# Layer 0 of a two-layer diffusion block: background sums moved into the merge, splits of two k tiles at a time, another order of the first eight blocks, an output product in five parts

## The chip, the cores and the metric

The kernel runs on one core of a Trainium2 chip. The metric is the device time of one execution in microseconds (us), the median over the runs shown. The core has TensorE (PE, matmuls), VectorE (DVE), ScalarE (ACT), GpSimd (POOL) and SyncE (SP); each works through a queue of its own in order, and SP's queue issues nearly all DMAs.

## The reference, cut to what matters

Two layers over 512 latent tokens and 256 context tokens of width 1024; the context goes through layer 0 in full and in layer 1 gives only keys and values. In each layer:

```
mod = silu(cond) @ w_mod[l] + b_mod[l]                      # six sections of 1024, for c and for c_ctx
h   = rms_norm(x) * (1 + scale1) + shift1
...                                                          # projection, conv mixer, attention, gMLP
x   = x + gate1 * (g_a*y_a + g_b*y_b + g_c*y_c) @ w_o        # the merge, then w_o
h2  = rms_norm(x) * (1 + scale2) + shift2
x   = x + gate2 * (silu(h2 @ w_ff1) * (h2 @ w_ff3)) @ w_ff2  # width 2816 = 22 tiles of 128
```

## The kernel before, in words

Everything is stored with the width on the 128 partitions and the tokens along the free axis, so an activation is eight k tiles of 128 x 768 in layer 0 (tokens 0 to 511 latent, XS; 512 to 767 context, CS) and of 128 x 512 in layer 1. Every GEMM keeps f32 accuracy by splitting both sides into a high and a low part: ACT casts the high part (`wh`, or the first half of `A`, `B`, `u`, `z`), and POOL or DVE subtracts it from the source for the low part (`split`, L223 to L225). A k tile costs three matmuls (`mm`, L227 to L235). A weight piece of 128 x 512 comes by one DMA on SP into `ws` (5 buffers), then becomes `wh` and `wl` (4 buffers each).

**Background sums.** The modulation vectors are sums over `w_modT`: one 512 KB tile (`wm`, 3 buffers) by DMA, then one DVE pass for each condition (`mod_sums`, L151 to L157), so two for the 32 tiles of layer 0's sections 2 to 5 and the first 16 of layer 1, and one for the last 32. They are called a few at a time by `pump`. A tiny POOL copy from a result of the place where the sum was called (`gate_mods`, L180) into the `wm` buffer holds the DMA back until that result exists.

**Merge, w_o, norm.** The merge takes eight output tiles j (`merge_b`, L821 to L830), with three sums behind each. The product with w_o (`wo_j`, L849 to L866) does tiles 0 to 3 over all 768 tokens, with two sums behind each, then tiles 4 to 7 over the token half 0 (0 to 383) and again over half 1 (384 to 767), so that the norm of half 0 runs while half 1 is multiplied (`lagged`, L417 to L431). `norm_half` (L400 to L415) writes the normed half as `Y` tiles (DVE multiplies, ACT adds the shift), and splits each into `A`.

**FF.** The first two of the 22 width tiles (`first_pair`, L898 to L924) are eight blocks of 24 matmuls: width tile n (0, 1), factor i (0 for w_ff1, 1 for w_ff3), half t. Its order is, written n,i,t: 000, 010, 001, 011, 100, 110, 101, 111. Beside it DVE forms sums and differences of `Y` (`pair_forms`, L282 to L297: `tf`, split into `B`), which the other ten pairs of width tiles need. Such a pair is `ff_pair` (L926 to L970): two products of seven matmul blocks in place of eight (`pair_product`), with weights that DVE adds up first (`fw`, L263), each product followed by one sum. The output product `ff2_j` (L985 to L1001) is taken in six parts of the width, 2, 4, 4, 4, 4 and 4 tiles; each part adds its product into the residual `xr` (DVE, L990) for all eight output tiles j. After each odd j a sum is called. In the last part, tiles j 0 to 3 run over all tokens, then 4 to 7 over XS, then 4 to 7 over CS, and the norm of layer 1 follows.

The order of the instructions on each engine is laid down when the kernel is built, by a scheduler that simulates a timeline; it differs from the order of the code.

Of the kernel before, what the change touches and what calls it, by code (L numbers as in the profile page):

```python
# [36 lines left out]
def dit_block(ctx: ExitStack, tc: tile.TileContext, xT, conds, vecs, ident_in, rope_c, rope_s,  # L37
# [27 lines left out]

# [210 lines left out]
    def half_of(k, t):  # L276
        return pair_at(8 * (k // 2) + 4 * t + 2 * (k % 2))

    def sum_of(i, kk):
        return pair_at(32 + 8 * i + 2 * kk)  # L280

    def pair_forms(Y, kk):  # L282

        b11, b12, b21, b22 = Y[kk, 0], Y[kk, 1], Y[kk + 4, 0], Y[kk + 4, 1]

        def form(x, y, op):
            t = slot("tf", HT)
            nc.vector.tensor_tensor(t, x, y, op=op)
            return t
        if kk % 2 == 0:  # L290
            new_arena(*range(8 + kk // 2, 16, 2))
# [108 lines left out]
    def norm_half(X, G, S, t, Y):  # L400

        a, b = t * HT, (t + 1) * HT
        RB = norm_stats(X, a, b)
        yield
        if t == 0:
            for kk in range(4):
                Y[kk, 0], Y[kk, 1], Y[kk + 4, 0], Y[kk + 4, 1] = four("Y")
        for k in (0, 4, 1, 5, 2, 6, 3, 7):
            y = Y[k, t]
            for u, v, c in kinds(a, b):  # L410
                nc.vector.scalar_tensor_tensor(y[:, u - a:v - a], X[k][:, u:v], G[:, k, c:c + 1], RB[:, u - a:v - a],
                                               op0=ALU.mult, op1=ALU.mult)
                nc.scalar.activation(y[:, u - a:v - a], y[:, u - a:v - a], AF.Identity, bias=S[:, k, c:c + 1])
            split(y, *half_of(k, t), nc.vector if k % 2 else nc.gpsimd)
            yield  # L415
# [45 lines left out]
    for l in range(2):  # L461
# [387 lines left out]
        def wo_j(j, sg):  # L849
# [48 lines left out]
        def first_pair(U):  # L898
# [14 lines left out]

            for n in range(2):
                for t in range(2):
                    for i in range(2):
                        if t == 0:
                            ww[n, i] = load_w(w_13[l, i, n], KD)
                        go(n, i, t)
                    if n == 1:  # L920
                        pair_forms(Y2, 2 * t)
                        pair_forms(Y2, 2 * t + 1)
# [48 lines left out]

        parts = [(0, 8), (8, 15), (15, 22)] if last else [(0, 2), (2, 6), (6, 10), (10, 14), (14, 18), (18, 22)]
        for pi, (f0, f1) in enumerate(parts):
# [11 lines left out]
            def ff2_j(j, sg):  # L985
# [87 lines left out]
```

## Time and profile before

| | us |
|---|---|
| median of the runs | 1975.67 (1975.33 to 1978.29, 3 runs) |
| the profiled execution's own time | 1975.22 |
| its span in the profile | 1973.4 |
| PE busy | 1879.8 (95% of the span) |
| DVE busy | 1164.6 (59%) |
| ACT busy | 747.8 (38%) |
| POOL busy | 859.9 (44%) |

The stages that the change touches, on the profile's clock: the merge from about 340 to 573 us, w_o from 573 to 643, `first_pair` to 693, the FF pairs and the output parts to 1183, then the norm of layer 1, whose first matmul starts at 1193. PE's busy share is the figure to start from; the places where PE waits or runs at a lower clock are read from the rows further down.

### The profile page before, as it was taken

Reading aid. Unit: us, or ns where it says so; the run is one execution under the profiler, and the core shown is the slowest. Engines: PE = TensorE matmul, PEld = TensorE weight load, DVE = VectorE, ACT = ScalarE, POOL = GpSimd, SP = SyncE. Lnnn points to the kernel's source line nnn. Section 1 sums busy time; section 2 is a strip of 40 time slices with the busy share of each in tenths; the row PEclk is TensorE's granted clock in tenths of the full one; section 3 lists DMA queues with packets and bytes.
Section 4 is the critical chain, followed back from the end, with each engine's and each line's share of the span. In section 5 each row is a group of like instructions: output and inputs, shape, how many; then the busy total and the mean of one; then the engine's idle time right before and its main releaser. Section 6 shows DMA issues by size and latency. Waiting matters only on the chain.

```text
span 1973.4 us, 27588 instructions
## 1 busy us (share of the span) xinstructions
PE 1879.8 (95%) x10150; PEld 1654.6 (84%) x10150; DVE 1164.6 (59%) x1936; ACT 747.8 (38%) x1459; POOL 859.9 (44%) x722
## 2 busy tenths in 40 slices
PE   5789999999999899999999998999999999999999
PEld 3578998888889789899999987888888888888887
DVE  7877865535359887877676867549523362322222
ACT  4346765222223623232322345448533352313121
POOL 4678743534334415152433347854333253424232
PEclk9989999999999899999999998999999999999999
DMA  8933201324255142323323354410322433332311
GB/s 280 306 101 97 76 27 39 134 76 149 75 185 195 38 144 91 129 91 118 119 95 134 119 183 153 135 34 5 107 90 92 147 108 127 100 102 86 111 43 66
DMA packets 107735, 222.42 MB, mean 113 GB/s; under 512 B 12368, under 2 KB 19792, under 8 KB 107600
## 3 DMA queue, kind: packets, MB, share of 16 engines
q1 hardware_dynamic: 105536, 217.51, 33.0%
q10 hardware_dynamic: 2064, 3.15, 0.6%
q8 instruction: 80, 1.31, 0.3%
q14 instruction: 55, 0.45, 0.1%
HBM read 212.74 MB, written 5.24 MB: 110 GB/s over the span
## 4 chain that ended last, share of the span: by engine, by line
PE 73%; DVE 14%; issue 4%; ACT 3%; DMA 3%; POOL 2%; ACTq 0%; SPq 0%; DVEq 0%; POOLq 0%
PE wide L234 33%; PE pD L234 21%; PE pD L311 5%; PE wide L311 5%; PE pF L234 3%; DMA wm<-in_w_modT 2%; DVE wm L156 2%; PE pO L765 2%; DVE wl L225 2%; PE pPT L759 1%; PE wide L733 1%; DVE junk L156 1%; DVE nm L737 1%; DVE nacc L352 1%; DVE ptl L762 1%
## 5 line engine op out<-in xcount | busy, mean ns | idle before, releaser
L225 POOL TENSOR_TENSOR wl<-ws,wh 128x512 fp32r<-128x512 f32 (+2 forms) x338 | 484.4, 1445 | 462.5 <-ACT wh L224 376.0
L234 PE MATMUL wide<-A,wh 128*128 128x512 f32 (+2 forms) x1728 | 469.3, 367 | 17.4 <-ACT A L224 8.2
L234 PEld LDWEIGHTS wide<-A,wh 128*128 128x128 f32 x1728 | 302.8, 192 | 72.7 <-ACT A L224 10.2
L224 ACT CAST wh<-ws 128x512 fp32r<-128x512 f32 (+2 forms) x536 | 302.2, 607 | 65.4 <-issue 17.5
L234 PE MATMUL wide<-A,wl 128*128 128x512 f32 (+2 forms) x864 | 289.1, 366 | 4.9 <-POOL wl L225 4.9
L225 DVE TENSOR_TENSOR wl<-ws,wh 128x512 fp32r<-128x512 f32 (+1 forms) x198 | 168.4, 851 | 131.5 <-ACT wh L224 121.5
L234 PE MATMUL pD<-A,wh 128*128 128x512 f32 (+1 forms) x784 | 238.2, 384 | 6.6 <-ACT A L224 2.8
L156 DVE SCALAR_TENSOR_TENSOR wm<-wm,fixed 128x1024 f32<-128x1024 f32 x112 | 152.1, 1361 | 49.4 <-DMA wm<-in_w_modT 47.5
L234 PEld LDWEIGHTS wide<-A,wl 128*128 128x128 f32 x864 | 154.2, 192 | 30.7 <-POOL wl L225 6.3
L234 PEld LDWEIGHTS pD<-A,wh 128*128 128x128 f32 x784 | 147.3, 193 | 35.0 <-ACT A L224 3.2
L234 PE MATMUL wide<-u,wh 128*128 128x512 f32 (+1 forms) x600 | 149.5, 352 | 0.9 <-DVE xr L990 0.9
L234 PE MATMUL pD<-A,wl 128*128 128x512 f32 (+1 forms) x392 | 148.7, 382 | 0.0
L234 PE MATMUL pD<-u,wh 128*128 128x512 f32 (+1 forms) x456 | 118.2, 357 | 0.0
L234 PEld LDWEIGHTS wide<-u,wh 128*128 128x128 f32 x600 | 98.9, 188 | 17.3 <-DVE xr L990 1.2
L742 POOL TENSOR_SCALAR pp<-pp,nm 128x768 f32<-128x768 f32 (+1 forms) x80 | 66.8, 836 | 101.2 <-DVE nm L741 65.5
L225 POOL TENSOR_TENSOR u<-su,u 128x768 fp32r<-128x768 f32 (+1 forms) x44 | 72.4, 1655 | 85.2 <-ACT u L224 85.2
L803 ACT ACTIVATE gate<-wide 128x512 f32<-128x512 f32 (+1 forms) x56 | 26.7, 516 | 199.8 <-PE wide L234 199.2
L156 DVE SCALAR_TENSOR_TENSOR junk<-wm,fixed 128x1024 f32<-128x1024 f32 x48 | 68.2, 1420 | 54.3 <-DMA wm<-in_w_modT 47.2
L809 DVE SCALAR_TENSOR_TENSOR gate<-gate,pD 128x512 f32<-128x512 f32 (+1 forms) x45 | 25.6, 596 | 122.4 <-PE pD L234 99.8
L224 ACT CAST wh<-fw 128x512 fp32r<-128x512 f32 x80 | 48.5, 615 | 121.8 <-DVE fw L263 106.3
L224 ACT CAST u<-su 128x768 fp32r<-128x768 f32 (+1 forms) x44 | 31.7, 728 | 165.7 <-DVE su L885 93.9
L234 PE MATMUL wide<-u,wl 128*128 128x512 f32 (+1 forms) x300 | 89.4, 351 | 0.0
(248 smaller groups left out, 3827.0 us busy)
## 6 DMA issues: line engine op xcount, KB each, us to landing
ws<-in_w SPq DMA_DIRECT2D x252, 256.0 KB, 3.8
wm<-in_w_modT SPq DMA_DIRECT2D x112, 512.0 KB, 4.3
ws<-in_w_in SPq DMA_DIRECT2D x184, 256.0 KB, 2.9
ws<-in_w_o SPq DMA_DIRECT2D x48, 256.0 KB, 5.4
ws<-in_w_abc SPq DMA_DIRECT2D x32, 256.0 KB, 2.7
ws<-in_w_six SPq DMA_DIRECT2D x16, 192.0 KB, 4.5
xr<-in_xT SPq DMA_DIRECT2D x8, 384.0 KB, 7.6
ws<-in_w SPq DMA_DIRECT2D x16, 192.0 KB, 2.4
```

Of the source, the lines that this page charges most:

```text
L156: nc.vector.scalar_tensor_tensor(o, t, 1.0, sbc[:, c, :], op0=ALU.mult, op1=ALU.mult, accum_out=MOD[l][:, sec, b, c:c + 1])
L224: nc.scalar.copy(hi, src)
L225: (lo_eng or nc.gpsimd).tensor_tensor(lo, src, f(hi), op=ALU.subtract)
L234: nc.tensor.matmul(d[:, :b - a], lhsT=ww, rhs=aa[:, a:b], start=kk == 0 and i == 0, stop=kk == n - 1 and i == 2)
L311: nc.tensor.matmul(D, lhsT=x[:, kk * P:(kk + 1) * P], rhs=a, start=kk == 0 and i == 0, stop=kk == 3 and i == 2)
L352: nc.vector.tensor_tensor(acc[:, :n], acc[:, :n], sq[:, :n], op=ALU.add)
L733: nc.tensor.matmul(D[:, a - k0:b - k0], lhsT=q[:, c * P - q0:(c + 1) * P - q0], rhs=kt[:, a:b], start=i == 0, stop=i == 1)
L737: nc.vector.tensor_reduce(nm[:, 0:1], D[:, :nk], axis=AX.X, op=ALU.max, negate=True)
L742: nc.gpsimd.tensor_scalar(pt[:, :nk], pt[:, :nk], nm[:, 3:4], 0.0, op0=ALU.mult, op1=ALU.add)
L765: nc.tensor.matmul(o[:, 0:256], lhsT=v3[:, kt, :], rhs=pp[:, j * 256:(j + 1) * 256], start=gi == 0 and j == 0 and i == 0, stop=gi == len(k ...
L803: nc.scalar.activation(g_[:, a:e], D, AF.Tanh, scale=0.5)
L809: nc.vector.scalar_tensor_tensor(g_[:, a:e], g_[:, a:e], 1.0, D, op0=ALU.add, op1=ALU.mult)
```

## The change

The diff, cut to its core (line numbers after it are two to seven higher than before: L910 of before is L914 after, L990 is L992, L413 is L419, L374 is L378):

```diff
@@ pair_forms, norm_half: two k tiles at a time @@
+    def split_two(t, u, eng):
+        d = arena[u // 4].rearrange("p (v h n) -> p h v n", h=2, n=HT)
+        split(t, d[:, 0], d[:, 1], eng)
...
-        t0 = form(b11, b12, ALU.subtract)
-        t1 = form(b22, t0, ALU.add)
-        t2 = form(b22, b12, ALU.subtract)
-        t3 = form(b21, t1, ALU.subtract)
-        for i, t in enumerate((t0, t1, t2, t3)):
-            split(t, *sum_of(i, kk), nc.vector)
+        nc.vector.tensor_tensor(ta, y[:, 0:4:3], y[:, 1:2].to_broadcast([P, 2, HT]), op=ALU.subtract)
+        nc.vector.tensor_tensor(tb[:, 0], y[:, 3], ta[:, 0], op=ALU.add)
+        split_two(ta, 32 + 8 * kk, nc.vector)
+        nc.vector.tensor_tensor(tb[:, 1], y[:, 2], tb[:, 0], op=ALU.subtract)
+        split_two(tb, 36 + 8 * kk, nc.vector)
...
-            split(y, *half_of(k, t), nc.vector if k % 2 else nc.gpsimd)
+            split_two(y4[:, t:4:2], 8 * kk + 4 * t, nc.vector if kk % 2 else nc.gpsimd)
@@ merge_b @@
-                pump(3)
+                pump(4)
@@ wo_j @@
-            if j < 4 and not last:
-                gate_mods[0] = Xn[j][:, W - 1:W]
-                pump(2)
@@ first_pair @@
-            for n in range(2):
-                for t in range(2):
-                    for i in range(2):
...
-                keep_u(su[n], U)
-                pump()
+            for n, i, t in ((0, 0, 0), (0, 1, 0), (1, 0, 0), (0, 0, 1), (0, 1, 1), (1, 0, 1), (1, 1, 0), (1, 1, 1)):
+                if t == 0:
+                    ww[n, i] = load_w(w_13[l, i, n], KD, "xx" if (n, i) == (1, 0) else "hl")
+                go(n, i, t)
...
@@ output product @@
-        parts = ... [(0, 2), (2, 6), (6, 10), (10, 14), (14, 18), (18, 22)]
+        parts = ... [(0, 4), (4, 8), (8, 12), (12, 16), (16, 22)]
...
-                if not last and j % 2:
+                if not last and f1 < NFF:
                     gate_mods[0] = X[j][:, W - 1:W]
                     pump()
...
-                lagged(ff2_j, segs, halves, lambda p: norm(X, G1[1], MOD[1][:, 0], *p, hnext))
+                lagged(ff2_j, segs, halves, lambda p: norm(X, G1[1], MOD[1][:, 0], *p, hnext), KD)
```

So all 32 tiles of layer 0's sums run in the merge, none in w_o and `first_pair`; behind each of the first four output parts stand eight sums in place of four, and behind the last none; the last part runs all eight j over XS first, then all eight over CS, and loads its weights for each. A fourth kind of weight tile (`wx`, 4 buffers) holds the piece that the third block of `first_pair` needs. The matmuls are the same in number and shape.

What this moves in the order of the engines is shown at three places. First ACT's queue in `first_pair`, where the L910 or L914 rows end a block of factor 0 (they read its PSUM bank), the L413 or L419 rows add the shift to `Y` tiles of half 1, and `A`, `B` and `wh` are casts. Before:

```order
L224 CAST A_5671<-Y_6219 128x384
L224 CAST B_6662<-tf_6682 128x384
L224 CAST wh_6590<-ws_6588 128x512
L224 CAST B_6663<-tf_6684 128x384
L224 CAST wh_6596<-ws_6594 128x512
L224 CAST wh_6627<-ws_6625 128x512
L224 CAST B_6664<-tf_6686 128x384
L910 ACTIVATE su_6453<-wide0_72 128x384
L224 CAST wh_6633<-ws_6631 128x512
```

After the change, the same stretch:

```order
L224 CAST A_5714<-Y_6216 128x2x384
L419 ACTIVATE Y_6217<-Y_6217,fixed_74 128x256
L419 ACTIVATE Y_6217<-Y_6217,fixed_74 128x128
L419 ACTIVATE Y_6217<-Y_6217,fixed_74 128x256
L914 ACTIVATE su_6438<-wide0_72 128x384
L419 ACTIVATE Y_6218<-Y_6218,fixed_74 128x128
L419 ACTIVATE Y_6218<-Y_6218,fixed_74 128x256
```

Before, the L910 shown is that of the first block over half 1, behind half 1's last `A` cast, and no L910 stands among half 1's shifts; after, the L914 of the third block over half 0 stands among them, and a cast of `A` or `B` takes two k tiles (128x2x384).

Second, DVE's queue around the end of the first output part, where L990 or L992 adds into `xr`, L156 is a sum (`wm` and `junk` are the two conditions of a tile), and `fw` and `wl` belong to the weights of the next pair. Before, after the part of two tiles:

```order
L990 SCALAR_TENSOR_TENSOR xr_6073<-pD_6941,fixed_74,xr_6073 128x512
L990 SCALAR_TENSOR_TENSOR xr_6073<-pD_6942,fixed_74,xr_6073 128x256
L156 SCALAR_TENSOR_TENSOR wm_6835,fixed_74<-wm_6835,fixed_74 128x1024
L156 SCALAR_TENSOR_TENSOR junk_6886,fixed_74<-wm_6883,fixed_74 128x1024
L990 SCALAR_TENSOR_TENSOR xr_6073<-wide0_72,fixed_74,xr_6073 128x512
L990 SCALAR_TENSOR_TENSOR xr_6073<-wide0_72,fixed_74,xr_6073 128x256
L225 TENSOR_TENSOR wl_7002<-fw_6999,wh_7001 128x512
L225 TENSOR_TENSOR wl_7012<-fw_7009,wh_7011 128x512
L225 TENSOR_TENSOR wl_7016<-fw_6993,wh_7015 128x512
L156 SCALAR_TENSOR_TENSOR wm_6883,fixed_74<-wm_6883,fixed_74 128x1024
L156 SCALAR_TENSOR_TENSOR junk_6932,fixed_74<-wm_6929,fixed_74 128x1024
L263 TENSOR_TENSOR fw_7019<-fw_6999,ws_6991 128x512
```

After the change, at the end of the part of four tiles:

```order
L992 SCALAR_TENSOR_TENSOR xr_6073<-wide1_73,fixed_74,xr_6073 128x512
L992 SCALAR_TENSOR_TENSOR xr_6073<-wide1_73,fixed_74,xr_6073 128x256
L156 SCALAR_TENSOR_TENSOR wm_7193,fixed_74<-wm_7193,fixed_74 128x1024
L156 SCALAR_TENSOR_TENSOR junk_7236,fixed_74<-wm_7233,fixed_74 128x1024
L992 SCALAR_TENSOR_TENSOR xr_6073<-pD_7323,fixed_74,xr_6073 128x512
L992 SCALAR_TENSOR_TENSOR xr_6073<-pD_7324,fixed_74,xr_6073 128x256
L225 TENSOR_TENSOR wl_7386<-fw_7383,wh_7385 128x512
L225 TENSOR_TENSOR wl_7390<-fw_7367,wh_7389 128x512
L156 SCALAR_TENSOR_TENSOR wm_7233,fixed_74<-wm_7233,fixed_74 128x1024
L156 SCALAR_TENSOR_TENSOR junk_7274,fixed_74<-wm_7271,fixed_74 128x1024
L263 TENSOR_TENSOR fw_7393<-fw_7373,ws_7365 128x512
L328 TENSOR_TENSOR tp_7403<-tp_7403,pD_7417 128x384
```

Behind the part's last evacuation seven passes of sums follow within the pair before, and nine after the change; ahead of it stand five before and eleven after.

Third, DVE's queue at the end of layer 0: L352 or L356 adds squares, `ms` and `RR` are the norm's factors, and L374 or L378 writes the normed tiles of layer 1. Before:

```order
L990 SCALAR_TENSOR_TENSOR xr_6073<-pD_11551,fixed_74,xr_6073 128x256
L352 TENSOR_TENSOR nacc_11571<-nacc_11571,nsq_11585 128x256
L357 TENSOR_SCALAR ms_11453<-pst_11448 128x4
L352 TENSOR_TENSOR nacc_11571<-nacc_11571,nsq_11588 128x256
L352 TENSOR_TENSOR nacc_11571<-nacc_11571,nsq_11591 128x256
L357 TENSOR_SCALAR ms_11597<-pst_11594 128x2
L362 COPY RR_11457<-rr_11455 128x512
L156 SCALAR_TENSOR_TENSOR wm_11493,fixed_74<-wm_11493,fixed_74 128x1024
L362 COPY RR_11601<-rr_11599 128x256
L374 SCALAR_TENSOR_TENSOR ny_11464<-xr_5684,fixed_74,pRB_11459 128x512
L374 SCALAR_TENSOR_TENSOR ny_11469<-xr_5684,fixed_74,pRB_11459 128x512
L374 SCALAR_TENSOR_TENSOR ny_11498<-xr_5837,fixed_74,pRB_11459 128x512
```

After the change:

```order
L992 SCALAR_TENSOR_TENSOR xr_5862<-wide1_73,fixed_74,xr_5862 128x256
L356 TENSOR_TENSOR nacc_11581<-nacc_11581,nsq_11586 128x256
L992 SCALAR_TENSOR_TENSOR xr_5862<-pD_11430,fixed_74,xr_5862 128x256
L225 TENSOR_TENSOR wl_11486<-ws_11483,wh_11485 128x512
L378 SCALAR_TENSOR_TENSOR ny_11317<-xr_5733,fixed_74,pRB_11312 128x512
L378 SCALAR_TENSOR_TENSOR ny_11322<-xr_5733,fixed_74,pRB_11312 128x512
L378 SCALAR_TENSOR_TENSOR ny_11359<-xr_5862,fixed_74,pRB_11312 128x512
L378 SCALAR_TENSOR_TENSOR ny_11364<-xr_5862,fixed_74,pRB_11312 128x512
L356 TENSOR_TENSOR nacc_11581<-nacc_11581,nsq_11589 128x256
L225 TENSOR_TENSOR wl_11519<-ws_11516,wh_11518 128x512
L992 SCALAR_TENSOR_TENSOR xr_5993<-wide1_73,fixed_74,xr_5993 128x256
L992 SCALAR_TENSOR_TENSOR xr_5993<-pD_11495,fixed_74,xr_5993 128x256
```

Before, all L990 rows are through ahead of the first normed tile; after, L992 rows of the CS pass (128x256) stand before and behind the normed tiles of XS, with the low parts of the pass's weights between them.

## Rows read from the trace of the kernel before

**Rows 1.** The page's first line.
```profile
span 1973.4 us, 27588 instructions
```

**Rows 2.** Stretches: length, then each engine's busy us (instructions), granted clock, DMA.
```profile
core 0: us, PE busy (x) PEld busy (x) DVE busy (x) ACT busy (x) POOL busy (x), PEclk, DMA share, GB/s
340.00:573.00 233.00, 233.00 (x1322) 202.27 (x1322) 100.26 (x147) 53.84 (x108) 97.20 (x83) 1.00 0.31 108
600.00:627.00 27.00, 25.49 (x146) 24.03 (x145) 27.00 (x42) 7.79 (x15) 13.74 (x9) 1.00 0.77 263
643.30:692.80 49.50, 41.64 (x202) 37.75 (x202) 39.78 (x77) 28.72 (x68) 21.01 (x15) 0.90 0.11 34
674.00:680.00 6.00, 5.79 (x18) 5.79 (x19) 6.00 (x7) 0.87 (x2) 4.28 (x4) 0.50 0.12 21
680.00:692.80 12.80, 12.80 (x75) 12.80 (x74) 8.00 (x17) 4.92 (x12) 1.65 (x2) 0.99 0.23 84
717.40:725.00 7.60, 7.60 (x35) 7.60 (x36) 7.60 (x13) 2.10 (x4) 1.21 (x2) 0.78 0.47 142
775.00:809.00 34.00, 34.00 (x198) 30.07 (x197) 21.95 (x36) 6.46 (x11) 13.16 (x13) 1.00 0.32 109
1178.00:1182.00 4.00, 4.00 (x34) 3.87 (x33) 4.00 (x7) 1.99 (x4) 2.12 (x1) 1.00 0.80 267
1193.30:1199.50 6.20, 6.06 (x15) 4.36 (x16) 6.20 (x8) 4.46 (x7) 5.58 (x7) 0.54 0.41 120
```

**Rows 3.** Waits of PE, 573 to 693 us: total, times, longest.
```profile
PE wide L234 <- POOL wl L225: 3.1, 2, 2.5
PE wide L234 <- ACT A L224: 2.4, 1, 2.4
PE wide L234 <- DVE xr L861: 1.5, 1, 1.5
```

**Rows 4.** Groups of ACT by line, 643 to 693 us and whole run.
```profile
L224 ACT CAST A<-Y 128x384 fp32r<-128x384 f32 x14 | 6.9, 501 | 0.0
L224 ACT CAST B<-tf 128x384 fp32r<-128x384 f32 x16 | 7.8, 510 | 4.2 <-DVE tf L288 4.1
L224 ACT CAST u<-su 128x768 fp32r<-128x768 f32 x22 | 18.1, 836 | 71.8 <-POOL su L952 27.8 <-PE wide L311 20.4 <-PE pD L311 11.9
```

**Rows 5.** Waits of PE, 693 to 1150 us.
```profile
PE wide L311 <- DVE xr L990: 3.4, 1, 3.4
PE pD L311 <- DVE wl L225: 2.4, 1, 2.4
PE pD L311 <- DVE tp L330: 2.2, 2, 1.1
```

**Rows 6.** Groups of DVE by shape, and SP's queue at 805 us.
```profile
L156 DVE SCALAR_TENSOR_TENSOR junk<-wm,fixed 128x1024 f32<-128x1024 f32 x48 | 68.2, 1420 | 54.3 <-DMA wm<-in_w_modT 47.2 <-PE wide L234 6.6 <-issue 0.5
L225 DVE TENSOR_TENSOR wl<-ws,wh 128x512 fp32r<-128x512 f32 x194 | 166.7, 860 | 130.7 <-ACT wh L224 120.8 <-issue 9.3
L263 DVE TENSOR_TENSOR fw<-fw,ws 128x512 f32<-128x512 f32 x40 | 38.2, 955 | 0.3
L990 DVE SCALAR_TENSOR_TENSOR xr<-wide,fixed,xr 128x512 f32<-128x512 f32 x41 | 30.6, 747 | 55.7 <-PE wide L234 55.7
805.51 9.88 SPq L153 DMA_DIRECT2D wm<-in_w_modT  x3
```

**Rows 7.** Timeline of PE at the end of layer 0: start, us.
```profile
1176.70 0.39 PE L234 MATMUL pD<-u,wl 128*128 128x512 f32 x1
1182.73 0.28 PE L234 MATMUL pD<-u,wl 128*128 128x256 f32 x1
1193.27 0.80 PE L234 MATMUL wide<-A,wh 128*128 128x512 f32 x1 [2.30 <-ACT A L224]
```

**Rows 8.** Timeline of DVE and POOL at 617 us.
```profile
618.09 1.77 DVE L225 TENSOR_TENSOR wl<-ws,wh 128x512 fp32r<-128x512 f32 x1
617.10 2.21 POOL L225 TENSOR_TENSOR wl<-ws,wh 128x512 fp32r<-128x512 f32 x1 [2.16 <-ACT wh L224]
```

More of the change, by code (lines that the diff above doesn't have):

```diff
@@ L203, in wtile, with load_w, load_piece @@
         return wp.tile([P, 512], F32 if kind == "s" else F32R, tag="w" + kind, name="w" + kind,
-                       bufs={"s": 5, "h": 4, "l": 4}[kind])
-    def load_w(src, nk):
+                       bufs={"s": 5, "h": 4, "l": 4, "x": 4}[kind])
+    def load_w(src, nk, kinds="hl"):
         res = []
         for k0 in range(0, nk, 4):
-            res += load_piece(src[:, k0:min(k0 + 4, nk), :].rearrange("p k n -> p (k n)"))
+            res += load_piece(src[:, k0:min(k0 + 4, nk), :].rearrange("p k n -> p (k n)"), kinds)
         return res
-    def load_piece(src):
+    def load_piece(src, kinds="hl"):
         n = src.shape[1]
@@ L218, in load_piece @@
         nc.sync.dma_start(st[:, :n], src)
-        hi, lo = wtile("h"), wtile("l")
+        hi, lo = wtile(kinds[0]), wtile(kinds[1])
         split(st[:, :n], hi[:, :n], lo[:, :n], eng)
@@ L276, in half_of, with two_forms @@
     def half_of(k, t):
-        return pair_at(8 * (k // 2) + 4 * t + 2 * (k % 2))
+        return pair_at(8 * (k % 4) + 4 * t + 2 * (k // 4))
     def sum_of(i, kk):
-        return pair_at(32 + 8 * i + 2 * kk)
+        return pair_at(32 + 8 * kk + 4 * (i % 2) + 2 * (i // 2))
+    def split_two(t, u, eng):
+        d = arena[u // 4].rearrange("p (v h n) -> p h v n", h=2, n=HT)
+        split(t, d[:, 0], d[:, 1], eng)
     def pair_forms(Y, kk):
[L284 to L291, printed above, removed]
-        t0 = form(b11, b12, ALU.subtract)
-        t1 = form(b22, t0, ALU.add)
-        t2 = form(b22, b12, ALU.subtract)
-        t3 = form(b21, t1, ALU.subtract)
-        for i, t in enumerate((t0, t1, t2, t3)):
-            split(t, *sum_of(i, kk), nc.vector)
+        y = Y[kk].rearrange("p (b n) -> p b n", n=HT)
+        new_arena(8 + 2 * kk, 9 + 2 * kk)
+        def two_forms():
+            t = big.tile([P, 2 * HT], F32, tag="tf", name="tf", bufs=2)
+            return t.rearrange("p (b n) -> p b n", n=HT)
+        ta = two_forms()
+        nc.vector.tensor_tensor(ta, y[:, 0:4:3], y[:, 1:2].to_broadcast([P, 2, HT]), op=ALU.subtract)
+        tb = two_forms()
+        nc.vector.tensor_tensor(tb[:, 0], y[:, 3], ta[:, 0], op=ALU.add)
+        split_two(ta, 32 + 8 * kk, nc.vector)
+        nc.vector.tensor_tensor(tb[:, 1], y[:, 2], tb[:, 0], op=ALU.subtract)
+        split_two(tb, 36 + 8 * kk, nc.vector)
     def four(name):
@@ L406, in norm_half @@
             for kk in range(4):
[L407 to L413, printed above, removed]
-            split(y, *half_of(k, t), nc.vector if k % 2 else nc.gpsimd)
+                Y[kk] = big.tile([P, 4 * HT], F32, tag="Y", name="Y", bufs=PAIRS["Y"])
+        for kk in range(4):
+            y4 = Y[kk].rearrange("p (b n) -> p b n", n=HT)
+            for k in (kk, kk + 4):
+                y = y4[:, 2 * (k // 4) + t]
+                for u, v, c in kinds(a, b):
+                    nc.vector.scalar_tensor_tensor(y[:, u - a:v - a], X[k][:, u:v], G[:, k, c:c + 1],
+                                                   RB[:, u - a:v - a], op0=ALU.mult, op1=ALU.mult)
+                    nc.scalar.activation(y[:, u - a:v - a], y[:, u - a:v - a], AF.Identity, bias=S[:, k, c:c + 1])
+                yield
+            split_two(y4[:, t:4:2], 8 * kk + 4 * t, nc.vector if kk % 2 else nc.gpsimd)
             yield
@@ L912, in go @@
                     nc.vector.tensor_tensor(o, o, D, op=ALU.mult)
-            for n in range(2):
-                for t in range(2):
-                    for i in range(2):
[L917 to L922, printed above, removed]
-                keep_u(su[n], U)
-                pump()
+            for n, i, t in ((0, 0, 0), (0, 1, 0), (1, 0, 0), (0, 0, 1), (0, 1, 1), (1, 0, 1), (1, 1, 0), (1, 1, 1)):
+                if t == 0:
+                    ww[n, i] = load_w(w_13[l, i, n], KD, "xx" if (n, i) == (1, 0) else "hl")
+                go(n, i, t)
+                if t == 1 and i == n:
+                    for kk in (2 * n, 2 * n + 1):
+                        pair_forms(Y2, kk)
+                if t == i == 1:
+                    keep_u(su[n], U)
         def ff_pair(m, U):
@@ L970, in ff_pair @@
             pump()
-        parts = [(0, 8), (8, 15), (15, 22)] if last else [(0, 2), (2, 6), (6, 10), (10, 14), (14, 18), (18, 22)]
+        parts = [(0, 8), (8, 15), (15, 22)] if last else [(0, 4), (4, 8), (8, 12), (12, 16), (16, 22)]
         for pi, (f0, f1) in enumerate(parts):
```

2 rows, old and new, of the table BUFS are left out of this document.

## The prediction

> **What bounds the kernel now.** I read the page first. The span is 1973.4 us [rows 1], and the profiled execution's own time, 1975.22, is 1.8 us more and 0.45 below the median of 1975.67, so what the sum moves in the span I take off 1975.22. PE is busy 95% of it, so PE is the bound almost everywhere: through the whole merge it has no gap, 233.00 of 233.00 us [rows 2]. A gain can come only from the places where PE waits or runs at a lower clock, and I looked for them stage by stage among the stages that the change touches.
>
> Three are worth the search. First, `first_pair`: 49.50 us [rows 2] for 192 matmuls. Near its end PE runs 75 of them in 12.80 us, 0.171 each [rows 2], so 192 need 32.8 and 16.7 us are lost. Waits for a weight's low part (3.1 us in all) and for `A` (2.4) are the largest named [rows 3]; and from 674 to 680 us the granted clock was 0.50, half of full speed, right behind the longest wait: 18 matmuls took 5.79 us in place of 3.1 [rows 2], 2.7 lost. Second, the end of layer 0: the last context matmul starts at 1182.73, the first matmul of layer 1 at 1193.27 [rows 7], and from there to 1199.50 the clock is 0.54 [rows 2]. Third, the FF pairs from 693 to 1150: the largest waits are 3.4, 2.4 and 2.2 (two of 1.1) [rows 5]; three more of about 1 us each bring them to 10.8, and behind the first the clock is 0.78: 35 matmuls took 7.60 us [rows 2] in place of 6.0, 1.6 lost. Together 12.4.
>
> **The change part by part.**
>
> *Merge.* Eight sums move in, one to each j, two DVE passes of 1.42 each [rows 6], 22.7 us. DVE is busy 100 of 233 us there [rows 2], so it has the room, and PE's unbroken 233 us of matmuls, 29 to a j, are the cover. The fourth sum's POOL copy waits for one of three `wm` buffers, for about one tile's two passes; behind it on POOL stand the low parts of the next j's weights, and behind its DMA on SP that j's pieces, both with a j of PE in front of them. If that cover fails, a PSUM evacuation waits for one pass or two: 0 to 22.7 us. PE has no gap at all with three sums behind each j, which is nearest to 0. I take 0.
>
> *w_o.* Eight sums leave, 22.7 us of DVE. From 600 to 627 us DVE was busy 27.00 of 27.00 [rows 2], and PE waited 1.5 us for one of its w_o evacuations [rows 3]. That wait goes: -1.5.
>
> *first_pair.* The first block over half 1 cannot end before half 1 is normed and split, whatever stands in front of it. Before, it was block 3, and five blocks of 24 x 0.171 = 4.1 us followed, 20.5, plus the wait and the clock (2.5 [rows 3] and 2.7), so it ended at about 692.8 - 25.7 = 667 us. After, a third half-0 block fills the wait, and four blocks follow: -4.1. The splits help a little: a cast of 2 x 384 should cost ACT 0.84 (its cast of 768) in place of 2 x 0.50, so half 1 has 4 x 0.17 = 0.7 us less of ACT, and `B`, 8 x 0.18 = 1.5 [rows 4]. Against it, `wx` adds nothing (the same pieces), but the next pair starts right behind this stage, where before the output part of two tiles gave DVE 18 us to finish `B`. So a wait at the pair's start is new; I give it 1.5 and count it under FF. The clock may well fall at the starved block as it does now. I take -3.5, between -0.5 (the wait is only moved) and -8 (the wait and the half clock go too). With w_o: -5.0.
>
> *FF pairs and output parts.* One part fewer saves DVE eight evacuations of 512 and of 256 (0.75 [rows 6] and some 0.47), 9.8 us, and PE the wait behind the two-tile part (3.4 [rows 5] plus 1.6 of clock). But each part now releases eight sums where it released four, on a DVE that is busy 21.95 of 34 us in such a part already [rows 2]. Four more two-pass sums are 11.4 us: 33 of 34 behind the first part, so what comes late spills into the next pair. There the order has nine passes behind the last evacuation, 12.8 us, ahead of or among weights (a pair product needs five `fw` at 0.96 and about six `wl` at 0.86 [rows 6], 10 us) against a pair product of 84 matmuls, 14.4 us of PE at 0.171. Before, seven such passes cost 3.4 + 1.6; nine, behind a longer part, cost I think 5.5 (3 to 9). The next three transitions have one-pass sums, 1.5 each (0 to 3). With 2.2 of waits for `tp` that I leave, and the 1.5 at the first pair, that is 13.7 against 12.4: +1.3. Bounds -5 and +8.
>
> *End of layer 0.* Before, 10.5 us lay between the last context matmul and layer 1 [rows 7], and the 15 matmuls to 1199.50 took 6.06 us [rows 2] where 15 x 0.226 = 3.4 would do (one of 512 and one of 256 columns take 34.00/99 = 0.343 at full clock, one of 256 takes 4.00/34 = 0.118 [rows 2]): 2.7 more, 13.2 together. After, the context pass is eight j of 18 matmuls at 0.118 us, 17.0 us behind the last XS evacuation, and the norm of XS runs under it; before, only 6 us of it did. The chain from the last XS matmul (1176.70) to layer 1's first took 16.6 [rows 7], which 17.0 just covers. What stays: the statistics' own matmuls, a wait for `RR`, a wait or two for weights whose parts stand behind normed tiles in DVE's and ACT's queues, some clock. I take 4.7 of 13.2, so -8.5. The context pass now loads weights of its own, 16 pieces by 16 DMAs, each cast and subtracted; if that slows it, all but 4 of the gain goes; if nothing waits, it is -12.
>
> Sum: 0 - 5.0 + 1.3 - 8.5 = -12.2, so **1963.0 us**.
>
> **A rule weighed against the trace.** A DVE subtraction of a `wl` that began at 618.09 beside a POOL subtraction (617.10 to 619.31) took 1.77 us against a mean of 0.86, and ended about half a microsecond behind it [rows 8, 6]. The Trainium skill's "SBUF — State Buffer", section "Who interferes with whom", says that a DVE instruction with two SBUF inputs and a GpSimd instruction that reads SBUF shut each other out for the whole instruction. The trace agrees. By that rule the longer splits on POOL hold DVE longer at a time, which is rival C.
>
> **The rivals.** *A, the sums pile up behind the output parts (slower).* The place is SP's queue: at 805.51 it took 9.88 us to issue three gated `wm` loads, with the next pair's weights behind them [rows 6], and the wait for a `wl` of 2.4 in that pair [rows 5] came of it. With eight sums there can be two or three such batches ahead of a weight piece, at four transitions. If each puts 9.88 us on PE, FF goes to 39.5 - 12.4 = +27.1 and the time to 1975.22 - 13.5 + 27.1 = 1988.8. It decides from (13.5 + 12.4)/4 = 6.5 us at a transition. Against it, DVE in such a part has 12 us free, and SP's wait of 9.88 cost PE only 2.4 us and one wait under 1. Chance 0.13.
>
> *B, the end of layer 0 gives little*, since ACT and DVE must make 16 weight pieces' parts and eight normed tiles in the same 17 us: gain 4 there, 1967.5; with half of FF's loss bound added, 1971. For it speaks that DVE was already busy 4.00 of 4.00 us at 1178 to 1182 [rows 2]; against it, its sums leave that stretch. Chance 0.18.
>
> *C, POOL's double splits hold DVE.* In `norm_half` half 1 gives POOL two splits of 2 x 384. At 2.21 us for 512 columns [rows 8], one of 768 columns is 3.3 us (estimate, in proportion); two of them in front of `B` on DVE put `B` and the first pair 6.6 us back: 1969.6. Against it, the forms have four blocks of PE, 16 us, in front of them. Chance 0.06.
>
> *D, more than I count:* the half clock and the 2.5 us wait in `first_pair` go, FF gains 5: 1963 - 4 - 6 = 1953. Chance 0.18. *E, nothing moves*, because what is covered in one place comes back in the next (DVE's work is the same but for 10 us): within 4 us of 1975. Chance 0.08. The forecast itself (1958 to 1968): 0.37.
>
> **The numbers.** About 0.2%, 4 us, is what a measurement can tell from no change. Forecast, D, C and nearly all of B lie more than 4 us below 1975.67: faster 0.77. E and a rest of B: same 0.10. A: slower 0.13. The range leaves out the far half of A and the tail beyond D: 1951 to 1976. The forecast's own is 1958 to 1968.
>
> **What would show it.** PE unbroken in the merge; no wait for w_o's evacuations; the span from the end of w_o to the first pair's first matmul some 4 us shorter, with one wait in it for half 1; a PE wait for `wl` or `fw` in the second pair, behind the part of four tiles, of 3 to 9 us, and none behind a two-tile part; the gap between the last context matmul and layer 1's first under 3 us, at a clock near 1. I am wrong if waits of PE after the four output parts sum to more than 20 us, if the context pass at the end takes well over 17 us, or if the merge shows gaps.

## The result and the profile after

| | before | after |
|---|---|---|
| median of the runs, us | 1975.5 (1974.44 to 1978.29, 4 runs) | 1953.21 (1951.87 to 1953.39, 4 runs) |
| ratio to before | | 0.9884, 95% interval 0.9866 to 0.9901 |
| span of the profiled execution | 1973.4 | 1950.0 |

The change made the kernel 22 us faster; 12.2 were forecast. 1953.2 lies in the range of 1951 to 1976, near its low end, and outside the forecast's own 1958 to 1968. To see where the 22 us came from I cut both profiled executions at the same matmuls (the start of a row in PE's timeline to the start, or for a last matmul the end, of another):

| stage, us | before | after | difference | forecast |
|---|---|---|---|---|
| up to the first matmul of w_o | 573.15 | 572.23 | -0.9 | 0 (merge) |
| w_o, to the first matmul on `A` | 70.16 | 68.20 | -2.0 | -1.5 |
| first_pair, to its last matmul | 49.65 | 41.73 | -7.9 | -3.5 |
| FF, to the last context matmul | 490.05 | 488.73 | -1.3 | +1.3 |
| gap to layer 1's first matmul | 10.26 | -0.17 | -10.4 | -8.5, this row and the next |
| start of layer 1, to the attention's first transpose | 125.68 | 127.32 | +1.6 | |
| from there to the end | 654.45 | 651.96 | -2.5 | 0 |

(The gap is negative since PE's rows overlap: the last context matmul is put down to end at 1170.89, and the next starts at 1170.72.) The first and the last row hold no instruction that the change moves out of its place on PE. Over the profiles of all fourteen kernels here the first lay between 572.2 and 575.8 (but for m8, below) and the last between 651.8 and 655.3, so some 3.5 us in each is what one execution differs from another by. In the kernels that leave them as the change has them, w_o repeats within 0.2 us and `first_pair` within 0.7, while the start of layer 1 lay between 126.2 and 129.3 in the seven kernels without a gap, so its +1.6 says little. The stages between the first row and the last give 20.0 us.

The page of the changed kernel: span, busy time with share and instructions, and the clock in 40 slices.

```profile
span 1950.0 us, 27698 instructions
...
PE 1868.8 (96%) x10150; PEld 1644.1 (84%) x10150; DVE 1178.3 (60%) x1910; ACT 750.5 (38%) x1455; POOL 868.6 (45%) x724
...
PEclk9989999999999999999999999999999999999999
```

PE is busy 11 us less than before for the same 10150 matmuls, its mean granted clock being 0.994 in place of 0.986, and it waits 12 us less. The stretches that answer to [rows 2], in the same columns:

```profile
core 0: us, PE busy (x) PEld busy (x) DVE busy (x) ACT busy (x) POOL busy (x), PEclk, DMA share, GB/s
340.00:573.00 233.00, 233.00 (x1324) 202.12 (x1323) 129.11 (x177) 53.37 (x106) 109.68 (x90) 1.00 0.35 124
600.00:627.00 27.00, 27.00 (x157) 26.20 (x156) 10.89 (x19) 10.76 (x23) 6.86 (x6) 1.00 0.23 82
640.40:682.00 41.60, 37.17 (x206) 34.30 (x204) 38.95 (x56) 24.35 (x47) 14.32 (x9) 1.00 0.10 32
674.00:680.00 6.00, 6.00 (x37) 6.00 (x36) 5.87 (x8) 1.67 (x3) 0.71 (x1) 1.00 0.01 3
757.00:800.00 43.00, 38.83 (x217) 37.46 (x218) 43.00 (x65) 15.56 (x27) 15.51 (x11) 1.00 0.35 117
1150.00:1170.70 20.70, 19.03 (x157) 18.62 (x156) 17.88 (x29) 13.29 (x28) 12.99 (x15) 1.00 0.64 199
1170.70:1177.00 6.30, 5.88 (x27) 4.52 (x26) 6.29 (x7) 4.04 (x8) 4.81 (x4) 1.00 0.81 269
```

The merge is as unbroken as before with 29 us more of DVE; from 600 to 627 us DVE has 10.89 us to do in place of 27.00; and PE runs 674 to 680 at full clock with 37 matmuls in place of 18. The waits of PE that answer to [rows 3], and under the dots to [rows 5]:

```profile
engine line waited for: us in total, times, longest us
PE wide L234 <- ACT su L914: 1.5, 2, 0.8
PE wide L234 <- POOL A L225: 1.3, 2, 0.6
PE pst L359 <- DVE nacc L356: 0.9, 1, 0.9
...
PE pD L315 <- DVE wl L225: 4.6, 4, 1.5
PE wide L315 <- DVE wl L225: 0.9, 1, 0.9
```

No wait in `first_pair` is over 1 us; before, there were two over 2. The waits for w_o's evacuation, for `tp` and behind the two-tile part are gone, and those for `wl` stand in their place, all but one in the second and third pair behind `first_pair`. There DVE is busy 43.00 of 43.00 us (757 to 800, above).

When the norm's factors reach PSUM (`pRB`), half 0 and then half 1, before:

```profile
638.46 0.49 PE L365 MATMUL pRB<-fixed,RR 128*128 128x128 f32 x3
654.68 0.49 PE L365 MATMUL pRB<-fixed,RR 128*128 128x128 f32 x3
```

After:

```profile
634.02 0.49 PE L369 MATMUL pRB<-fixed,RR 128*128 128x128 f32 x3
652.43 0.49 PE L369 MATMUL pRB<-fixed,RR 128*128 128x128 f32 x3
```

Half 0 is ready 4.4 us earlier and half 1 2.3 (0.9 us of each lies ahead of w_o). Last, PE's timeline at the end of layer 0, to be held against [rows 7]: the last XS matmul, two waits in the context pass, and the first matmul of layer 1.

```profile
1149.73 0.39 PE L234 MATMUL pD<-u,wl 128*128 128x512 f32 x1
...
1165.48 0.39 PE L234 MATMUL wide<-u,wl 128*128 128x256 f32 x1 [0.85 <-DVE wl L225]
1168.71 0.39 PE L234 MATMUL pD<-u,wl 128*128 128x256 f32 x1 [0.82 <-DVE wl L225]
...
1170.72 0.63 PE L234 MATMUL wide<-A,wh 128*128 128x512 f32 x2
```

Layer 1 follows the context pass with no gap. The pass took 20.9 us where 17.0 were forecast: its 144 matmuls, two waits of 0.8, and the statistics' matmuls. What it had to cover was done well before its end; ACT's first cast of `A` for layer 1, in ACT's timeline:

```profile
1162.37 0.62 ACT L224 CAST A<-ny 128x512 fp32r<-128x512 f32 x1
```

It ended 13.3 us behind the last XS matmul and 7.7 ahead of layer 1's first.

### The profile page after: what moved, and what is told of

Read it like the earlier page. It is cut to its first block, busy times and chain, and to the rows that moved or that the text cites. A ratio compares the mean times of both kernels' runs of the same rounds, so it can differ in the third digit from the quotient of the medians.

```text
span 1950.0 us, 27698 instructions
## 1 busy us (share of the span) xinstructions
PE 1868.8 (96%) x10150; PEld 1644.1 (84%) x10150; DVE 1178.3 (60%) x1910; ACT 750.5 (38%) x1455; POOL 868.6 (45%) x724
## 5 line engine op out<-in xcount | busy, mean ns | idle before, releaser
L225 POOL TENSOR_TENSOR wl<-ws,wh 128x512 fp32r<-128x512 f32 (+2 forms) x345 | 490.9, 1434 | 462.8 <-ACT wh L224 372.2
L234 PE MATMUL wide<-A,wh 128*128 128x512 f32 (+2 forms) x1696 | 455.6, 364 | 13.1 <-ACT A L224 3.3
L234 PEld LDWEIGHTS wide<-A,wh 128*128 128x128 f32 x1696 | 293.5, 189 | 65.7 <-ACT A L224 4.5
L224 ACT CAST wh<-ws 128x512 fp32r<-128x512 f32 (+2 forms) x546 | 306.7, 604 | 68.3 <-DMA ws<-in_w 13.2
L234 PE MATMUL wide<-A,wl 128*128 128x512 f32 (+2 forms) x848 | 281.1, 364 | 2.4 <-POOL wl L225 2.1
L225 DVE TENSOR_TENSOR wl<-ws,wh 128x512 fp32r<-128x512 f32 x201 | 173.6, 865 | 132.4 <-ACT wh L224 124.6
L156 DVE SCALAR_TENSOR_TENSOR wm<-wm,fixed 128x1024 f32<-128x1024 f32 x112 | 159.4, 1426 | 32.8 <-DMA wm<-in_w_modT 31.5
L234 PEld LDWEIGHTS wide<-A,wl 128*128 128x128 f32 x848 | 149.1, 190 | 28.1 <-POOL wl L225 3.6
L156 DVE SCALAR_TENSOR_TENSOR junk<-wm,fixed 128x1024 f32<-128x1024 f32 x48 | 70.5, 1468 | 61.3 <-DMA wm<-in_w_modT 60.8
L234 PEld LDWEIGHTS pD<-u,wh 128*128 128x128 f32 x464 | 79.0, 188 | 12.5
L234 PEld LDWEIGHTS pD<-A,wl 128*128 128x128 f32 x392 | 74.3, 190 | 14.6 <-POOL wl L225 0.8
```

Source lines behind the costliest of these rows:

```text
L156: nc.vector.scalar_tensor_tensor(o, t, 1.0, sbc[:, c, :], op0=ALU.mult, op1=ALU.mult, accum_out=MOD[l][:, sec, b, c:c + 1])
L224: nc.scalar.copy(hi, src)
L225: (lo_eng or nc.gpsimd).tensor_tensor(lo, src, f(hi), op=ALU.subtract)
L234: nc.tensor.matmul(d[:, :b - a], lhsT=ww, rhs=aa[:, a:b], start=kk == 0 and i == 0, stop=kk == n - 1 and i == 2)
```

## The experiments

Each kernel was run against the kernel before on the same chip, but not all on one chip. So a kernel is held against the change by its ratio to before (the change: 0.9884, 0.9866 to 0.9901) and by the stages of one profiled execution of each. First, one part of the change was undone at a time.

**u_last**: the last part in its old order.

```diff
-                lagged(ff2_j, segs, halves, lambda p: norm(X, G1[1], MOD[1][:, 0], *p, hnext), KD)
+                lagged(ff2_j, segs, halves, lambda p: norm(X, G1[1], MOD[1][:, 0], *p, hnext))
```

> The change with the last output part taken as before (four tiles over all tokens, then four over XS and four over CS), all else changed. Theory 1, the context pass of eight tiles covers the norm of layer 1: the gap between the last context matmul and layer 1 comes back almost whole, some 9 to 11 us slower than the changed kernel, near 1963. Theory 2, the gap closed because the sums left that stage and DVE had time: then most of the gain stays without the long pass, 2 to 5 us slower, near 1957.

1960.64 us, ratio 0.9924 (0.9903 to 0.9945). By stages, FF 484.8, the gap 2.8 and the start of layer 1 131.7: from the end of `first_pair` to the attention 619.4, against 615.9 in the change and 626.0 before. By these stages theory 2: 6.6 of the 10.1 us stay without the long pass. The whole run, 7.4 us above the change, lies between the theories; 3.6 us of the profiled execution's excess lie ahead of w_o, where the two kernels do the same. FF and the gap together are 0.9 us shorter than in the change; what the pass is worth lies in the start of layer 1 (131.7 for 127.3), whose first 15 matmuls take 5.9 us here and 3.6 in the change.

**u_sums**: the sums back in w_o, three behind each tile of the merge.

```diff
-                pump(4)
+                pump(3)
...
+            if j < 4 and not last:
+                gate_mods[0] = Xn[j][:, W - 1:W]
+                pump(2)
```

> The change with the sums back as they were in the merge (three behind each tile) and in w_o (two behind each of tiles 0 to 3). Theory 1, the sums in w_o held up the norm of half 0 by the 4.4 us by which its factors now come earlier, and PE for 1.5 us: 4 to 6 us slower than the changed kernel, near 1958. Theory 2, the order of the blocks alone fills first_pair, and what the sums delay is covered: 1.5 us slower (the wait in w_o), near 1955.

1958.61 us, 0.991 (0.9889 to 0.993). w_o 70.4 (+2.2), first_pair 42.6 (+0.9): 3.1 us, between the theories; the interval of the ratio overlaps the change's. Counted from the start of w_o, half 0's factors came 3.7 us later than in the change and half 1's 3.1, which is what the two stages lost.

**u_order**: two blocks over half 0 ahead of the first over half 1, as before.

```diff
-            for n, i, t in ((0, 0, 0), (0, 1, 0), (1, 0, 0), (0, 0, 1), (0, 1, 1), (1, 0, 1), (1, 1, 0), (1, 1, 1)):
+            for n, i, t in ((0, 0, 0), (0, 1, 0), (0, 0, 1), (0, 1, 1), (1, 0, 0), (1, 1, 0), (1, 0, 1), (1, 1, 1)):
...
```

> The change with the old order of the eight blocks (two over half 0 before the first over half 1, no wx). Theory 1, the third block keeps PE busy while half 1 is normed, and so its clock up: one block of 4.1 us and the 2.7 us of lower clock come back, 6 to 8 us slower than the changed kernel, near 1960. Theory 2, the earlier norm of half 0 and the paired splits are what shortened the stage: under 2 us slower, at most 1955.

1957.77 us, 0.991 (0.989 to 0.9931). first_pair 46.5, 4.7 longer than in the change. Its PE timeline has the wait for half 1 again:

```profile
658.92 1.01 PE L234 MATMUL wide<-A,wh 128*128 128x384 f32 x2 [3.28 <-ACT A L224]
```

and the stretches (columns as above) show what comes behind it:

```profile
655.00:660.00 5.00, 1.65 (x7) 0.87 (x5) 4.58 (x14) 3.74 (x10) 1.06 (x1) 0.79 0.01 2
660.00:665.00 5.00, 4.18 (x14) 4.18 (x15) 3.97 (x9) 5.00 (x12) 1.49 (x2) 0.53 0.01 0
```

PE was busy 1.65 of 5 us, and then ran at 0.53 of full speed while it was busy 4.18 of 5. In the change no stretch of that stage is below 1.00. So theory 1, with 4.7 us for 6 to 8 (the ratio alone does not part the two kernels). FF is 2.4 us shorter here than in the change.

**u_split**: each k tile split by itself.

```diff
-        split(t, d[:, 0], d[:, 1], eng)
+        for v in range(2):
+            split(t[:, v], d[:, 0, v], d[:, 1, v], eng)
```

> The change with each k tile split by itself again (ACT, DVE and POOL take twice as many instructions of half the size there; the forms stay in pairs). Theory 1, ACT and DVE bound half 1 and the forms, so fixed costs count: 1 to 3 us slower than the changed kernel, near 1955. Theory 2, POOL's longer splits held DVE by turns, so single ones are as fast or faster: 1951 to 1953.

1955.74 us, 0.9892 (0.9868 to 0.9915). The stage takes 41.8 us, as in the change (41.7). The groups of the low parts there, in the change (DVE's `B`, POOL's `A`: instructions, busy us, mean ns):

```profile
L225 DVE TENSOR_TENSOR B<-tf,B 128x768 fp32r<-128x768 f32 x8 | 8.5, 1076 | 2.4 <-ACT B L224 2.4
L225 POOL TENSOR_TENSOR A<-Y,A 128x768 fp32r<-128x768 f32 x4 | 8.2, 2038 | 9.8 <-ACT A L224 9.8
```

With single splits:

```profile
L225 DVE TENSOR_TENSOR B<-tf,B 128x384 fp32r<-128x384 f32 x16 | 10.6, 697 | 1.1 <-ACT B L224 1.0
L225 POOL TENSOR_TENSOR A<-Y,A 128x384 fp32r<-128x384 f32 x7 | 7.9, 1134 | 11.8 <-ACT A L224 9.8 <-DVE wl L225 2.1
```

DVE saves 2.1 us on `B` and POOL under 1 (the eighth single split starts ahead of the window), and neither reaches PE: the paired splits are worth 0.1 us here. For rival C, two rows of the change:

```profile
662.30 1.84 POOL L225 TENSOR_TENSOR A<-Y,A 128x768 fp32r<-128x768 f32 x1 [3.87 <-ACT A L224]
663.00 1.96 DVE L225 TENSOR_TENSOR B<-tf,B 128x768 fp32r<-128x768 f32 x1 [1.38 <-ACT B L224]
```

This `B` began inside POOL's split and took 1.96 us, where the others took 0.95, and ended 0.8 behind it. The Trainium skill's "SBUF — State Buffer", section "Who interferes with whom", says that a DVE instruction with two SBUF inputs and a POOL instruction that reads SBUF shut each other out. The trace agrees. So C's mechanism is there, but it held one `B` of eight, for 1.0 us in place of C's 6.6, and the stage's length does not show it.

**u_parts**: six output parts and, a second edit with it, a sum behind each odd tile; the long pass kept.

```diff
-        parts = ... [(0, 4), (4, 8), (8, 12), (12, 16), (16, 22)]
+        parts = ... [(0, 2), (2, 6), (6, 10), (10, 14), (14, 18), (18, 22)]
...
-                if not last and f1 < NFF:
+                if not last and j % 2:
```

> The change with six output parts as before (2, 4, 4, 4, 4 and 4 tiles) and a sum behind each odd tile (four to a part, some in the last part too), the long context pass kept. Theory 1, eight sums behind a part of four tiles cost PE about what four behind a part of two did: FF (end of first_pair to last context matmul) within 2 us of the change's 488.7. Theory 2, the two-tile part and the sums in the last part were what cost PE: FF some 4 to 6 us longer, and the gap to layer 1 opens again by 2 us or more in spite of the long context pass. Whole run 1953 by the first, 1958 to 1961 by the second.

1969.41 us, 0.9964 (0.9951 to 0.9977): most of the gain is lost. FF itself is 486.5, no longer, but the gap opens to 12.2 us, more than before the change, with the long pass in place. Theory 2 for the gap, and for FF nearest to theory 1 (2.2 us shorter). No wait in the pairs around the two-tile part is over 1.1 us here, where the kernel before had 3.4.

Next, parts of the change alone on the kernel before.

**a_last**: only the long pass (the line of u_last, the other way round).

> The kernel before with only the long context pass at the end (all eight tiles over XS, then over CS). The gap between the last context matmul and layer 1 was 10.3 us, and 3.5 us came back in the change without the long pass. Theory 1, the pass alone covers the norm: the stage from the end of first_pair to the attention of layer 1 shrinks by 7 to 10 us, 1966 to 1969. Theory 2, the sums that sit in that stage before hold DVE, so the pass alone gives 2 to 4 us: 1972 to 1974.

1984.08 us, 1.0042 (1.0027 to 1.0057): slower, which neither theory said. The gap is 11.9 and the start of layer 1 131.5 us. DVE's timeline shows two sums (L156) ahead of the factors (L362):

```profile
1187.13 1.21 DVE L156 SCALAR_TENSOR_TENSOR wm<-wm,fixed 128x1024 f32<-128x1024 f32 x1
...
1190.07 1.21 DVE L156 SCALAR_TENSOR_TENSOR wm<-wm,fixed 128x1024 f32<-128x1024 f32 x1
...
1192.67 0.42 DVE L362 COPY RR<-rr 128x512 f32<-128x512 f32 x1
```

and PE waited for these factors:

```profile
1193.14 1.11 PE L365 MATMUL pRB<-fixed,RR 128*128 128x128 f32 x4 [6.23 <-DVE RR L362]
```

**a_order**: only the order of the eight blocks, with `wx`.

> The kernel before with only the new order of the eight blocks (three over half 0 first, with wx). Undone in the change it cost 4.7 us in that stage. Theory 1, it works by itself: first_pair 4 to 6 us shorter than 49.65 and no stretch at half clock, 1970 to 1972. Theory 2, with the sums still in w_o the third block ends before half 1 is ready and PE waits as long: less than 2 us shorter, 1974 or more.

1977.36 us in ten runs from 1972.51 to 1982.22, 1.001 (0.9998 to 1.0021): no change. Yet first_pair was 43.2 us, 6.5 shorter, and at full clock from 657 us on. FF was 2.8 longer, the gap 1.0, the start of layer 1 5.8: all was given back: theory 1's stage with theory 2's time. The instructions from `first_pair` to the start of layer 1 stand in another order there, though the code of the stages behind `first_pair` is the same, since the scheduler lays them down anew. That this order is what gave the time back is not shown by itself.

**a_end**: a sum behind every tile of the first five parts, none in the last.

```diff
-                if not last and j % 2:
+                if not last and f1 < NFF:
```

> The kernel before with a sum behind every tile of the first five output parts and none in the last (the last part's own order, and all else, as before). The long context pass alone made that end 7 us longer, and the change without the pass kept 6.6 of its 10 us there. Theory 1, what closes the gap to layer 1 is that no sums sit in the last part: the stage from the end of first_pair to the attention of layer 1 shrinks from 626.0 by 3 to 7 us, and a rest of the gap, 3 to 6 us, stays; 1969 to 1973. Theory 2, both edits are needed together: within 2 us of 626.0, and 1974 or more.

1983.42 us, 1.0034 (1.0023 to 1.0044): slower again, which neither theory said. The gap fell to 7.0, but FF grew by 6.6 to 496.6 (eight sums stand behind the two-tile part, and the two pairs behind it took 73.5 us in place of 65.6) and the start of layer 1 to 131.9; 635.5 in all.

**a_both**: the edits of a_last and a_end together.

> The kernel before with both edits to the end of layer 0 and none of the others: a sum behind every tile of the first five output parts, none in the last part, and the long context pass. Alone, the first made the stage from the end of first_pair to the attention of layer 1 635.5 us, the second 634.9, against 626.0. Theory 1, the two only work together: the gap to layer 1 falls from 10.3 us to 1 or less, and gap plus the start of layer 1 from 135.9 to 127 to 130, while FF pays some 6 us for eight sums behind the two-tile part; 1973 to 1978. Theory 2, the change's part of six tiles (a context pass of 17 us in place of 11.5) is what closes it: a gap of 4 us or more stays.

1982.65 us, 1.0035 (1.0022 to 1.0047). The gap is 4.2, so theory 2: the part of six tiles is needed too, as far as two kernels show it that also differ ahead of FF. PE's timeline, the first matmul of layer 1 and one 60 us later:

```profile
1192.47 0.79 PE L234 MATMUL pD<-A,wh 128*128 128x512 f32 x1 [4.15 <-ACT A L224]
...
1252.24 0.80 PE L234 MATMUL pD<-A,wl 128*128 128x512 f32 x1 [4.17 <-POOL wl L225]
```

The second wait, of 4.17 us for a low part on POOL, has no counterpart before; waits of 2.0 to 3.7 us for POOL's `wl` stand near that place in u_last, u_parts, a_last, a_order and a_end as well. In these six kernels the start of layer 1 is 131 to 135 us; PE waits 4.0 to 6.5 us in it, 2.0 to 4.2 of them this wait, at a mean clock of 0.95 to 0.97 (before: 0.8 us, 0.98).

Last, since waits for `wl` in the second and third pair were what FF had left, and the merge's DVE had room, **m5h, m7 and m8** put more sums into the merge: five and six by turns, seven (shown) and eight to a tile.

```diff
-                pump(4)
+                pump(7)
```

> The change with eight sums behind each merge tile in place of four, so that all two-pass sums and half of the one-pass sums run in the merge (68 us more of DVE there, beside 123 of 233). Theory 1, the merge has room and what is left of the FF waits goes with the sums: the merge and w_o unchanged, FF waits of PE 4 us or less in place of 7.8, 2 to 5 us faster than the change, near 1949. Theory 2, the merge's evacuations or its DMA queue fall behind: PE gaps in the merge, more than 1956.

> The change with five and six sums by turns behind the merge's tiles (12 more sums in the merge, all of two passes, 34 us of DVE; eight to a tile made PE wait 5.5 us for evacuations there and fall to a lower clock once, and shortened FF by 9.7). Theory 1, with 18 us of DVE to a tile of 29 us the merge stays unbroken and FF shortens by 3 to 6 us: 1947 to 1950. Theory 2, the merge's evacuations already wait behind six passes in a row: a wait or two of over 1 us in the merge, no faster than the change.

> The change with seven sums behind each tile of the merge (24 more, 16 of them of two passes). Theory 1, between the others: FF shortens by 7 to 9 us and the merge loses 2 to 5, 1947 to 1950. Theory 2, the merge loses as much as with eight: 1951 or more.

m8: 1951.38 us, 0.9879 (0.9862 to 0.9895), between the theories. FF is 479.1, 9.7 shorter, but the merge lost 7.2 of that; its wait of PE, and its stretch:

```profile
PE wide L234 <- DVE gate L816: 5.5, 3, 3.7
```
```profile
340.00:582.00 242.00, 235.72 (x1335) 204.53 (x1334) 189.47 (x274) 55.02 (x108) 138.30 (x118) 0.99 0.52 180
```

m5h: 1953.57 us, 0.9877 (0.9858 to 0.9896), FF 486.6: like the change, though the merge had no wait, so neither theory. m7: **1947.78 us, 0.9849 (0.9834 to 0.9864)**, theory 1, and below both kernels. Its FF waits and stretches:

```profile
PE pD L315 <- DVE wl L225: 1.4, 2, 1.2
```
```profile
340.00:575.00 235.00, 235.00 (x1338) 204.00 (x1337) 179.81 (x263) 54.87 (x109) 131.81 (x112) 1.00 0.48 169
757.00:800.00 43.00, 43.00 (x250) 43.00 (x249) 38.17 (x57) 18.72 (x34) 15.11 (x12) 1.00 0.31 104
```

Seven sums leave the merge unbroken at 179.81 us of DVE in 235; with eight an evacuation is late. FF is 480.6, and the second and third pair have no wait, DVE being busy 38.17 of 43 us there.

## Why the prediction was right, and where it was not

The direction and the places were right, and the range held the time. The forecast itself, with 0.37, did not come: what came is rival D, with 0.18. It said that `first_pair` gives 4 us more and FF 5 in all, 1953, and by the prediction's own borders these two gave 7.9 (D: 7.5) and 4.8. By its steps:

*Merge, 0, and w_o, -1.5.* Right: no gap in the merge, and w_o 2.0 us shorter with its wait gone. u_sums shows that these are the sums: 2.2 us come back.

*first_pair, -3.5: mis-sized, measured -7.9.* I took one block of 4.1 us off and supposed that the clock "may well fall at the starved block as it does now". It did not fall. In that step's own terms, the first block over half 1 ended 21.4 us into the stage before and 22.8 after, and behind it five blocks took 28.3 us before and four took 19.0 after. That is 9.3 less: the block of 4.1, and the 2.5 of wait and 2.7 of clock that I had left standing. I had also seen only one of two drops of the clock: besides the 0.50 behind the wait for POOL's `wl`, the kernel before has one behind the wait of 2.4 us for half 1 (columns as above):

```profile
660.00:665.00 5.00, 4.66 (x20) 4.58 (x20) 4.44 (x11) 5.00 (x14) 1.89 (x3) 0.69 0.00 0
```

u_order brings back that one: with two blocks in front, PE waits 3.3 us for half 1 and then runs at half clock; with three, neither. The wait of 2.5 us for POOL's `wl`, and the half clock behind it, are gone in u_order and in a_order alike; what took them away is not shown. Undone, the order costs 4.7 us, the sums 0.9 and the splits 0.1, 5.7 of the 7.9; alone on the kernel before the order gave 6.5. My bound of -8 had this case in it ("the wait and the half clock go too").

*FF, +1.3: measured -1.3 in the table, and -4.8 by my own borders.* I had booked what the context pass loses under the end of layer 0, and the table's row holds it. Up to the last XS matmul FF took 483.7 us before and 467.6 after, and 96 context matmuls (11.3 us at 0.118) moved behind that point: -4.8. The term for the second pair was right: the two pairs behind the first part took 64.6 us where pairs without waits take 58.4, so 6.2 against my 5.5. The others were too high: 3.3 at the next three transitions for 4.5, 0.9 in the first pair for 1.5, and the 2.2 of waits for `tp` that I left standing are gone. What I counted as the gain of fewer parts is not theirs: on the same count u_parts, with six parts, has 479.3 where the change has 478.9 and the kernel before 483.7. Nor does it come back where w_o's sums, the order or the splits alone are undone (476.6 to 478.8), so what gives the 4.8 us stays open. Rival A, the queue behind gated loads, did not come: the waits of over 0.2 us in all pairs sum to 6.

*End of layer 0, -8.5: right in size, but the reason was incomplete.* By my own borders, what is lost behind the last XS matmul, over 0.118 us for each context matmul, fell from 10.9 us to 4.0, and the first 15 matmuls of layer 1 took 3.6 us in place of 6.6: -9.9. The rest of the start of layer 1 was 4.7 longer, which I had not in the sum; PE waits 3.8 us there in place of 0.8. I had the context pass cover the norm's chain, and named the sums' leaving only as a point against rival B. In the kernels run, the gap is closed only where three edits stand together. The pass, and the time from the last XS matmul to layer 1, by kernel:

```
                                              pass   to layer 1   gap (from the start of the last context matmul)
before: short pass, 4 tiles, sums in it        6.0    16.6         10.5
a_end:  short pass, 4 tiles, no sums           6.7    14.0         7.3
u_last: short pass, 6 tiles, no sums           9.6    12.7         3.1
a_last: long pass, 4 tiles, sums in it        12.2    24.3         12.1
u_parts: the same within the change           12.5    25.0         12.5
a_both: long pass, 4 tiles, no sums           12.9    17.4         4.4
change: long pass, 6 tiles, no sums           20.9    21.0         0.1
```

Where a gap is left, the middle column is the norm's chain. The long pass brings weights and evacuations of its own to DVE, and with four tiles the chain that it is to cover is longer for it, by 3 us without sums and by 8 with them. With six tiles it is hardly so: 12.7 in u_last, and 13.3 to the first cast of `A` in the change. (Six tiles and the long pass with sums left in were not run.) "The chain ... took 16.6, which 17.0 just covers" fitted by luck: the chain became shorter, and the pass longer. My sign of being wrong, a pass well over 17 us, came with 20.9; its 3.9 us are lost in the pass, and the gap did not need them.

*Rivals.* D came, as said. C's price is refuted by u_split, A by the waits, B by the gap.

## What to carry to other kernels

Undone one at a time, every part but the splits cost 3 us or more by the stages (the parts and their sums were undone together); alone on the kernel before, the order gave nothing, and the long pass, the sums behind every tile and these two together each made it slower (the sums' move and the five parts were not run alone). A cover must be longer than the chain as it will be with the cover's own work on the engines, so price the chain anew. And where a matmul engine starves, count the clock: before, the wait of 2.5 us in `first_pair` cost 2.7 more by what PE ran at behind it.

## What the runs showed of the hardware

The granted clock fell after some starved stretches, not after every wait: behind 1.65 busy us in 5 the next 5 ran at 0.53 (u_order), while behind the waits of 0.8 us each in the change it stayed at 1.00; yet in a_order, with no wait over 1.1 us, 7 us ran at 0.79 behind 4.82 busy us in 7. A DVE subtraction that began inside a POOL split took 1.96 us for 0.95. Ten executions of a_order spread over 10 us and fourteen of the kernel before over 7, where the four of the change lay within 1.5. Where the waits for POOL's `wl` at the start of layer 1 come from, in the kernels where the code of that stage is the same, stays open: the order of POOL and ACT there differs from before in all of them, but also in kernels without such a wait, and I did not vary it by itself.
